# Three pairs of FFN blocks by seven products, two weight sums by adding transfers, another end and narrower masks in a decoder layer in float32

## The chip, the cores and the metric

The kernel runs on one core of a Trainium2 chip. What counts is the device time of one execution in microseconds (us). The core's engines each have their own instruction queue, worked off in order: TensorE (PE, its weight loads PEld), VectorE (DVE), ScalarE (ACT), GpSimd (POOL) and SyncE (SP, which here only issues transfers). Engines wait for each other by semaphores.

## The reference

One decoder layer on x of 256 positions and width 1024, all in float32: a half-step SwiGLU FFN, then attention in parallel with a gated MLP, then a second half-step FFN, a final norm; shift, scale and gate of each part come from a product of the conditioning vector c with `w_ada`.

```python
y = modulate(rmsnorm(h, norm_ffn2[l]), sh3, sc3)
h = h + 0.5 * gt3[:, None, :] * swiglu(y, w_ffn2_gu[l], w_ffn2_down[l])
return rmsnorm(h, norm_final)

def swiglu(x, w_gu, w_down):
    g, u = jnp.split(x @ w_gu, 2, axis=-1)
    return (jax.nn.silu(g) * u) @ w_down
```

The hidden width of an FFN is 2816. Sequence length equals the attention's block, so attention is causal within the 256 positions.

## The kernel before, in words

**Tiles.** The 256 positions are two tiles of 128 rows (t = 0, 1). A product in float32 is made of three TensorE products of a reduced type: each operand is split into a high part (a ScalarE copy into that type) and a low part (what is left, a VectorE subtraction), and high·high, low·high and high·low are summed in PSUM (`mm3`). A weight piece is 128 rows by 1024 columns (512 KB). SP loads it into one of 8 `raw` buffers (RBUFS), ScalarE writes `wh`, VectorE `wl`, of which there are 10 each (WBUFS). The pieces of `w_ada` (`ada`) use the same `raw` buffers.

**The second FFN** (`f2`) goes over 11 blocks of 256 hidden columns (NB). For each block there is a part that makes gate and up, an activation (silu on ScalarE, product on VectorE), a split of the result into `ah` and `al` (`turn`), and `down(b)`, 24 matmuls of 512 columns that add the block's share to four PSUM banks `po`. A plain block (`gate_up`) is 16 groups of six matmuls of 256 columns in banks `pg` and `pu`. The blocks named in PAIRS (line 33: 5 and 8) and the block after each are made together (`pair`, lines 549 to 614) by Strassen's scheme: with weights cut into quarters 11, 21 (first block, upper and lower half of the rows) and 12, 22 (second block), seven products P1, P5, P6, P2, P7, P3, P4 stand for eight. Each is 12 matmuls of 512 columns in one of three banks pA, pB, pC. P1, P6 and P7 accumulate in the same bank pA, and between them ScalarE copies it out (`copy`, line 571: u1 after P1, u2 after P6, u3 after P7), so P6 waits for u1 and P7 for u2. Silu for a pair's tiles is `gated` (line 576). A pair's results lie in another layout, so `turn` has TensorE transpose them (four transposes a block) before the split. The sums of activation parts that Strassen's scheme needs (`sum_y`: two VectorE instructions and a ScalarE copy each, four sums) are made once, in the plain blocks that `due` (line 1216) names.

**A pair's weights** (`add_pair`, lines 227 to 291): for each product and each half q of its rows, `prep` loads what is still needed, makes the weight sum by `minus` in place on VectorE (two for P5, four for P6, two after P2, for both q together), and `hi` writes the high part (line 242); `lo` writes the low part. Product n+1 is prepared before the low part of n. After P7 and after P4 a plain `down` follows (`pair_downs`), whose weights stand between the pair's.

**What sets the order.** While TensorE's instructions are written, `tick` calls `fillers` (line 391) whenever a model clock of VectorE is less than LEAD ahead of TensorE's: that issues the next weight, if fewer than WBUFS are live, or the next item of the conditioning (`fill`), at most one piece of `w_ada` per GAP. Each item puts its load on SP's queue, its high part on ScalarE's and its low part on VectorE's. Eight pieces of the last gate (`acc`) are summed by VectorE during the second FFN.

**The end** (lines 1240 to 1270): the downs of the last three blocks (HOLD) are done tile by tile and half by half (t, n). For the very last half the last block goes into two banks `pe` of 256 columns; `add` scales, adds to h, squares and multiplies with the final norm's row.

**Masks.** A causal mask of 128 by 128 (`make_mask`, lines 179 to 185) is added to the attention scores by a matmul with the identity; for t = 1 `maskr` holds a zero half ahead of it, so that the matmul writes all 512 columns of the bank (`step_sc`, line 1079).

## Time and profile before

| | |
|---|---|
| median of 3 runs | 500.62 us (500.24 to 501.04) |
| the profiled execution's own time | 500.92 us |
| its span, first to last instruction | 499.2 us |
| granted TensorE clock, mean | 0.994 of full speed |
| busy | TensorE 98%, VectorE 82%, ScalarE 56%, GpSimd 5% |
| data moved by transfers | 126.46 MB, mean 253 GB/s |

A profile is one execution. A busy share is the share of the span in which an engine worked on an instruction; consecutive records of VectorE and ScalarE overlap by a few hundredths of a microsecond, so n instructions in a row take a little less than n times one. The second FFN with its downs runs from about 310 us to 491 us of the span.

### The profile page before, as it was taken

The page shows a single profiled execution, that of the slowest core. Times are in us where ns is not written, and L with a number is a line of the kernel's source. Part 1 is how long each engine was busy: PE and PEld are TensorE (multiplying, and loading weights), DVE is VectorE, ACT ScalarE, POOL GpSimd, SP SyncE. Part 2 cuts the span into 40 slices and gives each one's busy share as a digit, 9 for nine tenths or more (in the row PEclk, how much of TensorE's full clock was granted, in tenths as well). Part 3 has the DMA queues.
Part 4 walks back from the last instruction along what each step waited for, and adds up shares of the span by engine and source line. Part 5 has one row for each costly group of instructions (what it writes and reads, how often), then busy time and mean ns, then how long its engine had stood idle before and what let it go on. Part 6 is the DMA issues. An engine that isn't in the chain of part 4 may idle for free.

```text
span 499.2 us, 7816 instructions
## 1 busy us (share of the span) xinstructions
PE 487.7 (98%) x2959; PEld 431.6 (86%) x2959; DVE 411.6 (82%) x537; ACT 277.9 (56%) x412; POOL 23.6 (5%) x36
## 2 busy tenths in 40 slices
PE   8999999999999999999999999999999999999993
PEld 6999998999999997887788988889998789788982
DVE  5999989897778557799888999879898879988345
ACT  5656775553544443775676447855536663766221
POOL 4000000000000200100003221000000000000000
PEclk9999999999999999999999999999999999999997
DMA  8999979998899975569776767697901982294002
GB/s 285 404 398 397 399 235 349 410 396 294 315 331 339 337 260 173 178 195 334 242 269 240 228 199 287 214 324 269 352 0 49 341 314 97 93 350 149 0 1 84
DMA packets 38023, 126.46 MB, mean 253 GB/s; under 512 B 4449, under 2 KB 4449, under 8 KB 37986
## 3 DMA queue, kind: packets, MB, share of 16 engines
q1 hardware_dynamic: 37458, 125.39, 70.2%
q10 hardware_dynamic: 432, 0.57, 0.3%
q8 instruction: 23, 0.38, 0.3%
q14 instruction: 14, 0.11, 0.1%
q0 software_dynamic: 96, 0.01, 0.0%
HBM read 124.91 MB, written 1.05 MB: 252 GB/s over the span
## 4 chain that ended last, share of the span: by engine, by line
PE 83%; DVE 7%; issue 4%; ACT 3%; DMA 3%; POOL 0%; POOLq 0%; ACTq 0%; DVEq 0%; SPq 0%
PE po L82 19%; PE pg L82 17%; PE pu L82 13%; PE f L82 6%; PE pw L82 4%; PE pA L82 3%; PE pp_gv L82 2%; PE pp_v L82 2%; PE pp_q L82 2%; PE pp_k L82 2%; PE pp_gu L82 2%; PE psc L82 2%; DMA raw_first<-in_gu_dram 2%; DVE raw_gu L82 1%; DVE wl_gu_5P L82 1%
## 5 line engine op out<-in xcount | busy, mean ns | idle before, releaser
L82 DVE TENSOR_TENSOR wl_gu<-raw_gu,wh_gu 128x1024 fp32r<-128x1024 f32 x56 | 66.9, 1221 | 11.5 <-ACT wh_gu L203 11.3
L203 ACT ACTIVATE wh_gu<-raw_gu 128x1024 fp32r<-128x1024 f32 x56 | 57.3, 1054 | 25.0 <-PE po L82 15.3
L82 PE MATMUL po<-wh_d,ah 128*128 128x512 f32 x174 | 68.3, 392 | 0.2 <-ACT ah L522 0.2
L82 PE MATMUL po<-wl_d,ah 128*128 128x512 f32 x174 | 68.4, 393 | 0.0
L82 PE MATMUL po<-wh_d,al 128*128 128x512 f32 x174 | 68.2, 392 | 0.0
L82 DVE TENSOR_TENSOR wl_d<-raw_d,wh_d 128x1024 fp32r<-128x1024 f32 x44 | 53.4, 1225 | 13.3 <-ACT wh_d L203 13.3
L203 ACT ACTIVATE wh_d<-raw_d 128x1024 fp32r<-128x1024 f32 x44 | 45.8, 1054 | 28.3 <-PE pu L82 10.3
L82 PE MATMUL pu<-yh,wh_gu 128*128 128x256 f32 x192 | 54.3, 283 | 0.3 <-DVE a L82 0.2
L82 PE MATMUL pg<-yh,wh_gu 128*128 128x256 f32 x192 | 54.5, 284 | 0.0
L82 PE MATMUL pu<-yh,wl_gu 128*128 128x256 f32 x192 | 54.4, 283 | 0.0
L82 PE MATMUL pg<-yh,wl_gu 128*128 128x256 f32 x192 | 54.4, 283 | 0.0
L82 PE MATMUL pu<-yl,wh_gu 128*128 128x256 f32 x192 | 54.2, 283 | 0.0
L82 PE MATMUL pg<-yl,wh_gu 128*128 128x256 f32 x192 | 54.2, 282 | 0.0
L82 PEld LDWEIGHTS po<-wh_d,al 128*128 128x128 f32 x174 | 32.7, 188 | 7.5 <-DVE al L82 0.4
L82 PEld LDWEIGHTS po<-wh_d,ah 128*128 128x128 f32 x174 | 32.7, 188 | 7.2 <-ACT ah L522 0.4
L82 DVE SCALAR_TENSOR_TENSOR ada<-ada,c_row 128x1024 f32<-128x1024 f32 x32 | 38.6, 1219 | 0.0
L82 PEld LDWEIGHTS po<-wl_d,ah 128*128 128x128 f32 x174 | 32.7, 188 | 6.6
L82 PEld LDWEIGHTS pu<-yh,wh_gu 128*128 128x128 f32 x192 | 36.3, 189 | 0.8 <-DVE a L82 0.4
L82 PEld LDWEIGHTS pg<-yh,wh_gu 128*128 128x128 f32 x192 | 36.3, 189 | 0.5
L82 PEld LDWEIGHTS pg<-yl,wh_gu 128*128 128x128 f32 x192 | 36.2, 188 | 0.5
L82 PEld LDWEIGHTS pu<-yh,wl_gu 128*128 128x128 f32 x192 | 36.2, 189 | 0.0
L82 PEld LDWEIGHTS pg<-yh,wl_gu 128*128 128x128 f32 x192 | 36.2, 189 | 0.0
(321 smaller groups left out, 1090.4 us busy)
## 6 DMA issues: line engine op xcount, KB each, us to landing
raw_gu<-in_gu_dram SPq DMA_DIRECT2D x72, 512.0 KB, 5.4
raw_d<-in_w_ffn_down_dram SPq DMA_DIRECT2D x44, 512.0 KB, 5.0
ada<-in_w_shsc_dram SPq DMA_DIRECT2D x32, 512.0 KB, 5.2
ada<-in_w_gate_dram SPq DMA_DIRECT2D x24, 512.0 KB, 5.5
raw_ada<-in_w_shsc_dram SPq DMA_DIRECT2D x16, 512.0 KB, 7.2
raw_first<-in_gu_dram SPq DMA_DIRECT2D x16, 512.0 KB, 7.5
raw_wo<-in_w_out_dram SPq DMA_DIRECT2D x8, 512.0 KB, 4.9
raw_inq<-in_w_in_dram SPq DMA_DIRECT2D x4, 512.0 KB, 5.5
```

The lines of the kernel that those rows point to most:

```text
L82: return getattr(self.engine, name)(out, *args, **kw)
L203: nc.scalar.activation(wh[:, :n], raw[:, :n], AF.Copy)
```

## The change

Pairs are now blocks 3+4, 6+7 and 9+10; 0, 1, 2, 5 and 8 are plain. In a pair's weights, the sums 22 − 12 (for P7) and 21 − 11 (for P4) are made by `less`: ScalarE negates a raw quarter in place (line 257) and GpSimd issues a transfer from one raw buffer to the other that adds (line 258); there are 12 of these in all. VectorE keeps four subtractions per pair of eight. Quarter 22 is loaded with P5's, 21 with P6's, and P4 uses the buffers of 11 rather than those of 21. All four activation sums are made in block 2. At the end, block 8 alone is left for `po` in the last half, and blocks 9 and 10 go into the two `pe` banks, twelve matmuls each; the turns of blocks 9 and 10 stand among the last downs. The mask matmul writes only the 128 columns per head of the tile's own keys, so for t = 1 it has 256 columns in place of 512 (four instructions), and `maskr` loses its zero half with the VectorE instruction that made it. The program has 98 matmuls and transposes fewer (rows of the order, 2802 to 2704), VectorE 483 to 489 instructions, ScalarE 347 to 370, GpSimd 41 to 53, SP 248 as before.

```diff
--- before.py
+++ after.py
@@ -30,7 +30,7 @@
 RBUFS = 8
 HOLD = 3
 AHEAD = 4
-PAIRS = (5, 8)
+PAIRS = (3, 6, 9)
 STRASSEN = ("P1", "P5", "P6", "P2", "P7", "P3", "P4")
 LEAD = 1
 GAP = 3
@@ -174,15 +174,14 @@
     vec.tensor_scalar(onesr, ident, 0.0, 1.0, op0=ALU.mult, op1=ALU.add)
     identr = const.tile([P, P], F32R, name="identr")
     vec.tensor_copy(identr, ident)
-    maskr = const.tile([P, 2, P], F32R, name="maskr")
+    maskr = const.tile([P, P], F32R, name="maskr")
 
     def make_mask():
         mask = op.tile([P, P], F32, name="mask", bufs=1)
         nc.gpsimd.memset(mask, 0.0)
         nc.gpsimd.affine_select(out=mask, in_=mask, pattern=[[-1, P]], base=0,
                                 channel_multiplier=1, compare_op=ALU.is_ge, fill=NEG)
-        vec.tensor_scalar(maskr[:, 0, :], mask, 0.0, None, op0=ALU.mult)
-        vec.tensor_copy(maskr[:, 1, :], mask)
+        vec.tensor_copy(maskr, mask)
 
 
 
@@ -253,18 +252,25 @@
         def minus(to, x, y, q):
             vec.tensor_tensor(part[to, q], part[x, q], part[y, q], op=ALU.subtract)
 
+        def less(to, x, q):
+
+            nc.scalar.activation(part[to, q], part[to, q], AF.Copy, scale=-1.0)
+            nc.gpsimd.dma_start(part[to, q], part[x, q], accum_op=ALU.add)
+
         def prep(key, q):
 
-            if q == 0 and key in ("P1", "P5", "P6", "P2"):
-                load(*{"P1": ("11", b, 0), "P5": ("12", b + 1, 0), "P6": ("22", b + 1, 1), "P2": ("21", b, 1)}[key])
+            if q == 0:
+                for name, blk, half in {"P1": (("11", b, 0),), "P5": (("12", b + 1, 0), ("22", b + 1, 1)),
+                                        "P6": (("21", b, 1),)}.get(key, ()):
+                    load(name, blk, half)
             if key == "P5":
                 minus("11", "12", "11", q)
+                less("12", "22", q)
             elif key == "P6":
-                minus("12", "22", "12", q)
                 minus("11", "22", "11", q)
             hi(place[key], key, q)
 
-        place = dict(zip(STRASSEN, ("11", "11", "11", "21", "12", "22", "21")))
+        place = dict(zip(STRASSEN, ("11", "11", "11", "21", "12", "22", "11")))
         order = [(key, q) for key in STRASSEN for q in range(2)]
 
         def item(n):
@@ -275,8 +281,8 @@
                     prep(*order[n + 1])
                 key, q = order[n]
                 lo(place[key], key, q)
-                if key == "P2":
-                    minus("21", "21", "11", q)
+                if key == "P6":
+                    less("11", "21", q)
             return run
 
         for n, (key, q) in enumerate(order):
@@ -1082,13 +1088,16 @@
         hb, par, h0 = sc_of(t, q)
         p = p_sc[t, q] = psa(f"psc{t}{q}").rearrange("p (h n) -> p h n", h=hb)
         rs = slice(par * DH, (par + 1) * DH)
-        mk = maskr.rearrange("p a b -> p (a b)")[:, 2 * P - nk:]
-        ten.matmul(p, identr, mk[:, None, :].to_broadcast([P, hb, nk]), start=True, stop=False)
+
+
+        ten.matmul(p[:, :, tsl(t)], identr, maskr[:, None, :].to_broadcast([P, hb, P]), start=True, stop=False,
+                   skip_group_check=True)
         for hh in range(hb):
             hd = h0 + 2 * hh + par
             for kk in range(t + 1):
                 ten.matmul(p[:, hh, tsl(kk)], qkT[0, t][rs, hd // 2, :],
-                           qkT[1, kk][rs, hd // 2, :], start=False, stop=(hh == hb - 1 and kk == t))
+                           qkT[1, kk][rs, hd // 2, :], start=False, stop=(hh == hb - 1 and kk == t),
+                           skip_group_check=True)
 
     def step_mx(t, q):
         once(("mx", t, q), ("sc", t, q))
@@ -1213,7 +1222,7 @@
         sums_y[m] = (zh, zl)
 
     waiting = [0, 1]
-    due = {2: [1], 3: [3], 4: [2, 4]} if min(PAIRS) > 4 else {2: [1, 3], 3: [2, 4]}
+    due = {2: [1], 3: [3], 4: [2, 4]} if min(PAIRS) > 4 else {2: [1, 3], 3: [2, 4]} if min(PAIRS) > 3 else {2: [1, 3, 2, 4]}
     for b in range(2, NB):
         if b in PAIRS:
             f2.pair(b, waiting, pair_downs(b))
@@ -1243,22 +1252,23 @@
 
         for n in range(2):
             apart = (t, n) == (NT - 1, 1)
-            for b in range(NB - HOLD, NB - 1 if apart else NB):
+            for b in range(NB - HOLD, NB - 2 if apart else NB):
                 if b == NB - 2 and last not in f2.a:
                     f2.turn(last)
                 for k in range(2):
-                    end = b == NB - 2 and k == 1 if apart else None
+                    end = b == NB - 3 and k == 1 if apart else None
                     run(f2.down_ops(b, k, t, end)[3 * n:3 * n + 3])
             add(n, f2.po[t][n], slice(0, 512), not apart)
         if apart:
             for q in range(2):
                 o = slice(q * 256, q * 256 + 256)
                 pe = psm(f"pe{q}")[:, 0:256]
-                for k in range(2):
-                    ah, al = f2.a[last]
-                    wh, wl = need(("d2", last, k))
-                    mm3(pe, ah[:, k, tsl(t)], al[:, k, tsl(t)], wh[:, 512 + o.start:512 + o.stop],
-                        wl[:, 512 + o.start:512 + o.stop], k == 0, k == 1)
+                for b in (NB - 2, NB - 1):
+                    for k in range(2):
+                        ah, al = f2.a[b]
+                        wh, wl = need(("d2", b, k))
+                        mm3(pe, ah[:, k, tsl(t)], al[:, k, tsl(t)], wh[:, 512 + o.start:512 + o.stop],
+                            wl[:, 512 + o.start:512 + o.stop], (b, k) == (NB - 2, 0), (b, k) == (NB - 1, 1))
                 add(1, pe, o)
             v = sm.tile([P, 1], F32, tag="var", name=f"v2_z{t}")
             vec.tensor_tensor(v, c.parts[0], c.parts[1], op=ALU.add)
```

The order of instructions follows from `fillers`. Three places show it. Names: `wh_gu2_5P31` is the high part for pair 5, product P3, second half (q = 1); `raw_gu2_6110` the raw quarter 11 of pair 6, first half; `u1_25` the copy u1 of pair 5; `d2_3_0` the first weight of block 3's down.

ScalarE in the second half of a pair's weights: before, pair 5 (line 571 is the copy of bank pA, 242 a pair's high part, 203 another weight's, 522 the split of a turned block).

```order
L242 ACTIVATE wh_gu2_5P21_4144<-raw_gu2_5211_4124 128x1024
L242 ACTIVATE wh_gu2_5P70_4160<-raw_gu2_5120_3963 128x1024
L242 ACTIVATE wh_gu2_5P71_4179<-raw_gu2_5121_3965 128x1024
L242 ACTIVATE wh_gu2_5P30_4186<-raw_gu2_5220_4002 128x1024
L571 ACTIVATE u1_25_4193<-pA25_4171 128x512
L522 ACTIVATE ah_24_4195<-a_24_4134 128x512
L203 ACTIVATE wh_d2_3_0_4206<-raw_d2_3_0_4205 128x1024
L203 ACTIVATE wh_d2_3_1_4218<-raw_d2_3_1_4217 128x1024
L242 ACTIVATE wh_gu2_5P31_4229<-raw_gu2_5221_4004 128x1024
L242 ACTIVATE wh_gu2_5P40_4236<-raw_gu2_5210_4122 128x1024
L571 ACTIVATE u2_25_4243<-pA25_4171 128x512
```

Now, pair 6 (577 the copy, 241 and 202 the high parts, 257 the negation).

```order
L241 ACTIVATE wh_gu2_6P20_4253<-raw_gu2_6210_4200 128x1024
L257 ACTIVATE raw_gu2_6111_4098<-raw_gu2_6111_4098 128x1024
L241 ACTIVATE wh_gu2_6P21_4265<-raw_gu2_6211_4202 128x1024
L241 ACTIVATE wh_gu2_6P70_4277<-raw_gu2_6120_4115 128x1024
L241 ACTIVATE wh_gu2_6P71_4287<-raw_gu2_6121_4117 128x1024
L241 ACTIVATE wh_gu2_6P30_4294<-raw_gu2_6220_4119 128x1024
L577 ACTIVATE u1_26_4298<-pA26_4272 128x512
L528 ACTIVATE ah_25_4300<-a_25_4228 128x512
L202 ACTIVATE wh_d2_4_0_4323<-raw_d2_4_0_4322 128x1024
L202 ACTIVATE wh_d2_4_1_4335<-raw_d2_4_1_4334 128x1024
L241 ACTIVATE wh_gu2_6P31_4343<-raw_gu2_6221_4121 128x1024
L577 ACTIVATE u2_26_4347<-pA26_4272 128x512
```

Ahead of u1 stand four high parts (P2's second half, both of P7, one of P3) as before, and now a negation ahead of those; between u1 and u2 stand the two weights of a down, as before, and one high part of the pair in place of two.

VectorE between two pairs: before, after pair 5.

```order
L82 TENSOR_TENSOR wl_d2_4_0_4275<-raw_d2_4_0_4273,wh_d2_4_0_4274 128x1024
L82 TENSOR_TENSOR wl_d2_4_1_4287<-raw_d2_4_1_4285,wh_d2_4_1_4286 128x1024
L82 TENSOR_TENSOR u3_25_4291<-u3_25_4291,pC25_4172 128x512
L82 TENSOR_TENSOR u3_25_4291<-u3_25_4291 128x256
L82 TENSOR_TENSOR wl_gu2_7_0_4319<-raw_gu2_7_0_4317,wh_gu2_7_0_4318 128x1024
L82 TENSOR_TENSOR wl_gu2_7_1_4327<-raw_gu2_7_1_4325,wh_gu2_7_1_4326 128x1024
L82 TENSOR_TENSOR wl_gu2_7_2_4338<-raw_gu2_7_2_4336,wh_gu2_7_2_4337 128x1024
L82 TENSOR_TENSOR wl_gu2_7_3_4356<-raw_gu2_7_3_4354,wh_gu2_7_3_4355 128x1024
L82 TENSOR_TENSOR wl_d2_5_0_4368<-raw_d2_5_0_4366,wh_d2_5_0_4367 128x1024
L82 TENSOR_TENSOR u2_25_4243<-u2_25_4243,pC25_4172 128x512
L82 TENSOR_TENSOR u2_25_4243<-u2_25_4243 128x256
L82 TENSOR_TENSOR wl_d2_5_1_4383<-raw_d2_5_1_4381,wh_d2_5_1_4382 128x1024
```

Now, after pair 3.

```order
L82 TENSOR_TENSOR wl_d2_2_0_3957<-raw_d2_2_0_3955,wh_d2_2_0_3956 128x1024
L82 TENSOR_TENSOR wl_d2_2_1_3970<-raw_d2_2_1_3968,wh_d2_2_1_3969 128x1024
L82 SCALAR_TENSOR_TENSOR acc8_3401<-ada8_4_3977,cols_79,acc8_3401 128x1024
L82 TENSOR_TENSOR wl_gu2_5_0_3988<-raw_gu2_5_0_3986,wh_gu2_5_0_3987 128x1024
L82 TENSOR_TENSOR u2_23_3877<-u2_23_3877,pC23_3809 128x512
L82 TENSOR_TENSOR u2_23_3877<-u2_23_3877 128x256
L82 TENSOR_TENSOR wl_gu2_5_1_4006<-raw_gu2_5_1_4004,wh_gu2_5_1_4005 128x1024
L82 TENSOR_TENSOR u4_23_4013<-u4_23_4013,pA23_3808 128x256
L82 TENSOR_TENSOR wl_gu2_5_2_4022<-raw_gu2_5_2_4020,wh_gu2_5_2_4021 128x1024
L82 SCALAR_TENSOR_TENSOR acc8_3401<-ada8_5_4031,cols_79,acc8_3401 128x1024
L82 TENSOR_TENSOR wl_gu2_5_3_4041<-raw_gu2_5_3_4039,wh_gu2_5_3_4040 128x1024
L82 TENSOR_TENSOR wl_d2_3_0_4053<-raw_d2_3_0_4051,wh_d2_3_0_4052 128x1024
```

Steps of `acc8`, the summing of the last gate, now stand between the weights there; before, all of them came ahead of the first pair.

TensorE where the last gate and up ends: before.

```order
L82 MATMUL pu210_4883<-yh_109,wh_gu2_10_3_4796 128x256
L82 MATMUL pu210_4883<-yl_110,wh_gu2_10_3_4796 128x256
L82 MATMUL pu210_4883<-yh_109,wl_gu2_10_3_4797 128x256
L82 MATMUL po200_3757<-wh_d2_8_0_4808,ah_28_4931 128x512
L82 MATMUL po200_3757<-wl_d2_8_0_4809,ah_28_4931 128x512
L82 MATMUL po200_3757<-wh_d2_8_0_4808,al_28_4932 128x512
L82 MATMUL po200_3757<-wh_d2_8_1_4823,ah_28_4931 128x512
```

Now.

```order
L82 MATMUL pA29_4749<-wl_gu2_9P41_4827,yh_109 128x512
L82 MATMUL pa_29_4948<-ident_99,u1_29_4773 128x128 x2
L82 MATMUL pa_29_4948<-ident_99,u4_29_4945 128x128 x2
L82 MATMUL po200_3774<-wh_d2_8_0_4836,ah_28_4775 128x512
L82 MATMUL po200_3774<-wl_d2_8_0_4837,ah_28_4775 128x512
L82 MATMUL po200_3774<-wh_d2_8_0_4836,al_28_4776 128x512
L82 MATMUL po200_3774<-wh_d2_8_1_4851,ah_28_4775 128x512
L82 MATMUL po200_3774<-wl_d2_8_1_4852,ah_28_4775 128x512
L82 MATMUL po200_3774<-wh_d2_8_1_4851,al_28_4776 128x512
L82 MATMUL pa_210_4965<-ident_99,u2_29_4821 128x128 x2
L82 MATMUL pa_210_4965<-ident_99,u3_29_4871 128x128 x2
```

Before, a plain block (`pu210`) stood ahead of the last downs; now P4 of pair 9 stands there, and the transposes of block 9, the second two of which read u4, which is made from P4's bank, come right behind it.

## Rows read from the trace of the kernel before

**Rows 1.** The page's part 1: busy us (share of the span), instructions, of each engine.

```profile
PE 487.7 (98%) x2959; PEld 431.6 (86%) x2959; DVE 411.6 (82%) x537; ACT 277.9 (56%) x412; POOL 23.6 (5%) x36
```

**Rows 2.** Table by stretches: PE, PEld, DVE, ACT, POOL busy; PEclk, DMA share, GB/s.

```profile
341.00:358.00 17.00, 17.00 (x123) 16.00 (x122) 16.04 (x17) 8.73 (x10) 0.00 (x0) 1.00 0.92 341
...
358.00:390.00 32.00, 32.00 (x190) 28.30 (x189) 28.22 (x29) 17.07 (x21) 0.00 (x0) 1.00 0.25 77
...
390.00:414.00 24.00, 23.81 (x106) 19.11 (x105) 19.85 (x22) 15.90 (x22) 0.00 (x0) 1.00 0.92 338
```

**Rows 3.** Chain of waits from 330 to 500 us: start, us, what.

```profile
341.73 5.51 PE po L82 x24
...
348.68 0.72 PE pg L82 x6
...
385.57 3.39 DMA raw_d<-in_w_ffn_down_dram
...
392.02 0.49 ACT u L571
...
431.91 2.79 PE pA L82 x12
...
466.64 0.44 PE pa L82 x4
```

**Rows 4.** VectorE's timeline, second FFN: start, duration, engine, operation, [idle before, releaser].

```profile
327.35 1.22 DVE L82 TENSOR_TENSOR wl_gu<-raw_gu,wh_gu 128x1024 fp32r<-128x1024 f32 x1
...
329.44 0.42 DVE L82 TENSOR_TENSOR a<-sg,pg 128x256 f32<-128x256 f32 x1 [0.87 <-ACT sg L500]
...
338.70 0.69 DVE L82 TENSOR_TENSOR s1l<-y_f,s1h 128x512 fp32r<-128x512 f32 x1 [0.70 <-ACT s1h L1211]
...
339.31 1.28 DVE L82 SCALAR_TENSOR_TENSOR acc<-ada,cols,acc 128x1024 f32<-128x1024 f32 x1
...
378.89 1.22 DVE L82 TENSOR_TENSOR wl_gu_5P<-raw_gu,wh_gu_5P 128x1024 fp32r<-128x1024 f32 x1
...
391.30 4.62 DVE L82 TENSOR_TENSOR wl_gu_5P<-raw_gu,wh_gu_5P 128x1024 fp32r<-128x1024 f32 x4
...
413.39 0.41 DVE L82 TENSOR_TENSOR u<-u,pA 128x256 f32<-128x256 f32 x1
...
427.05 2.35 DVE L82 TENSOR_TENSOR wl_gu_8P<-raw_gu,wh_gu_8P 128x1024 fp32r<-128x1024 f32 x2
```

**Rows 5.** TensorE's timeline: the first matmul of P1 of pair 5.

```profile
381.14 0.40 PE L82 MATMUL pA<-wh_gu_5P,yh 128*128 128x512 f32 x1
```

**Rows 6.** ScalarE's timeline, pair 5.

```profile
384.13 0.60 ACT L571 ACTIVATE u<-pA 128x512 f32<-128x512 f32 x1 [0.52 <-PE pA L82]
...
390.03 1.99 ACT L242 ACTIVATE wh_gu_5P<-raw_gu 128x1024 fp32r<-128x1024 f32 x2
...
412.89 0.36 ACT L576 ACTIVATE u<-pA 128x256 f32<-128x256 f32 x1
```

**Rows 7.** DMA issues: queue, count, KB each, median us from issue to landing.

```profile
raw_gu<-in_gu_dram SPq DMA_DIRECT2D x72, 512.0 KB, 5.4
...
acc<-in_b_ada_dram POOLq DMA_DIRECT2D x3, 4.0 KB, 4.8
```

**Rows 8.** TensorE's groups from 240 to 262 us: the mask's matmuls (t = 1).

```profile
L82 PE MATMUL psc<-maskr,identr 128*128 128x512 f32 x4 | 1.8, 445 | 0.0
```

**Rows 9.** VectorE's timeline at the end.

```profile
489.80 0.69 DVE L82 TENSOR_TENSOR res_z<-po,ada_row 128x512 f32<-128x512 f32 x1 [0.60 <-PE po L82]
...
491.13 0.42 DVE L82 TENSOR_TENSOR res_z<-pe,ada_row 128x256 f32<-128x256 f32 x1
...
492.38 0.42 DVE L82 TENSOR_TENSOR res_z<-pe,ada_row 128x256 f32<-128x256 f32 x1
```

**Rows 10.** GpSimd's timeline, 280 to 320 us.

```profile
297.38 1.46 POOL L415 TENSOR_TENSOR r_f<-v_f,mhalf 128x1 f32<-128x1 f32 x1 [9.80 <-DVE v_f L82]
...
310.35 0.56 POOL L415 TENSOR_TENSOR r_f<-v_f,mhalf 128x1 f32<-128x1 f32 x1 [9.72 <-DVE v_f L82]
```

## The prediction

> **What bounds the kernel now.** The page's first part comes first: TensorE is busy 98% of the span, VectorE 82%, ScalarE 56% [rows 1]. So a TensorE instruction removed is a gain only as long as the split weights arrive in time, and 82% is an average that has to be read stage by stage. The table by stretches does that for the second FFN [rows 2]: between 341 and 414 us TensorE is busy without a gap that counts, while VectorE is busy 16.04 of 17 us, 28.22 of 32 and 19.85 of 24. TensorE leads, and VectorE follows close behind with little room. How close, the timelines show. In pair 5 the low part of P6's second half starts on VectorE at 378.89 and ends at 380.1 [rows 4]; TensorE starts P1 of that pair at 381.14 [rows 5], so VectorE is 1.0 us ahead of P1. For pair 8 the same low part ends at 428.2 [rows 4] and P1 starts at 431.91 [rows 3]: 3.7 ahead. The one place where this lead was too short is in the chain: P7 of pair 5 waited for ScalarE's copy u2 of bank pA (392.02, 0.49 us [rows 3]). That copy stands in ScalarE's order behind weights' high parts [rows 6], one of which waited for its load (385.57, 3.39 us [rows 3]). The same order is kept by the change, so this is the place to watch.
>
> **What TensorE saves.** All of this is against the profiled execution, 500.92 us with a span of 499.2; it lies 0.3 above the median of the three runs and inside their spread, so no correction is made.
> - A plain block is 16 groups of six matmuls at 0.72 us, a product twelve at 2.79 [rows 3]. Two plain blocks, 32 × 0.715 = 22.9, become seven products, 19.5: −3.4. Two more blocks are turned by four transposes, 0.44 each [rows 3]: +0.9.
> - Four mask matmuls [rows 8] shrink from 512 to 256 columns, from 0.23 us (2.79/12) to 0.12 (0.72/6): −0.45. The VectorE instruction dropped from the opening is worth nothing beside other work there.
> - The end: six 512-column matmuls of `po` go into the two `pe` banks, so `po` ends 6 × 0.23 = 1.4 us earlier and VectorE's work on it (from 489.80) is done before the first `pe` arrives. TensorE's own end stays. The second piece starts on VectorE at 492.38 now, behind the first at 491.13 [rows 9]; it can start some 0.3 us after TensorE's last matmul, at about 491.15: −1.2.
> - Block 9's turn now stands right behind P4 of the last pair, and its operand is P4's own result: silu 0.36 on ScalarE [rows 6], product 0.41 on VectorE [rows 4], with handoffs about 1.1, less two transposes that are ready: +0.9. Before, a plain block stood in between.
>
> Sum: −3.4 + 0.9 − 0.45 − 1.2 + 0.9 = −3.3, or **497.6** if nothing comes late.
>
> **What the splitting costs.** Prices on VectorE, each less the 0.08 us by which its records overlap: 1024 columns 1.14 (four in 4.62, one alone 1.22), an `acc` step 1.20, 512 columns 0.61, 256 columns 0.34 [rows 4]. A high part on ScalarE is about 1.0, a copy of a bank 0.6 [rows 6].
>
> *Pair 3.* TensorE reaches P1 when block 2 and the downs of block 0 are done, 341.73 + 5.51 = 347.24 [rows 3] (0.45 earlier with the masks, for both engines alike), and ends P5 at 352.8. From 327.35 VectorE has ten instructions of 1024 columns, eleven of 512 and one of 256 up to and with P6's second low part: 11.4 + 6.7 + 0.35 = 18.45. All four activation sums are now among them. The waits it has now stay: 0.87 for the silu, 0.70 for ScalarE in each of four sums [rows 4], some 1.1 for high parts: 4.8. It is done at 350.6, 3.4 **after** P1's start where pair 5 had 1.0 before it. ScalarE can only then negate that half, and P2's and P7's high parts are queued ahead of copy u1: 3 × 1.0 + 0.6 and a handoff, 354.3. P6 accumulates in bank pA, so it waits for u1: stall 1.5.
>
> P7 waits for u2, and u2 stands behind the high part of the first weight of block 1's down. That weight's load takes the raw buffer which the fourth adding transfer reads. (Behind it in SP's queue stand that down's second weight and block 2's, which are read only after P7.) Negation done 351.7, the transfer L, the load 3.4 [rows 3], high part 1.0, copy 0.6, handoffs 0.5: 357.2 + L, against the end of P2 at 359.9. Stall L − 2.7.
>
> *L* has no row. A transfer issued by GpSimd takes 4.8 us to land even for 4 KB [rows 7]; 512 KB at the 341 GB/s of that stretch [rows 2] is 1.5 more. I take 6.3. Bounds: 3.4, a load by the other queue [rows 3], below; 4.8 + 5.4 = 10.2 [rows 7] above. With 6.3 the stall is 3.6. The Trainium skill, "DMA: Bandwidth & Descriptors", section "Anatomy of one DMA — SWDGE (gpsimd) path", puts a transfer on this path at 2.0 us plus bytes/436e3, by my estimate 3.2 for 512 KB; by that the total below would be 501.1. The 4.8 of rows 7, where it would give 2.0, speak against it here.
>
> *Pair 6.* From 350.6 VectorE has 28 × 1.14 + 5 × 1.20 (the `acc` steps now fall between pairs 3 and 6) + 7 × 0.61 + 4 × 0.34 = 43.5 until P6's second low part. Its idle share was 13% of its busy time at 358 to 390 and 21% at 390 to 414 [rows 2]: 5.8 to 9.1, so done between 399.9 and 403.2. TensorE: seven products, three downs, block 5 with two turns and the stalls so far, 347.24 + 19.5 + 16.5 + 12.3 + 5.1 = 400.7 for P1, 406.3 for P6. Here six ScalarE instructions stand from that low part to u1 (negation, four high parts, copy), 5.7 us: u1 at 405.6 to 408.9, stall 0 to 2.6, taken 1.5. P7's u2 stands behind the second weight of block 4's down, whose load waits for the eighth adding transfer, and one more high part: stall L − 3.7 = 2.6.
>
> *Pair 9.* No `acc` step is left and VectorE is ahead by several us, as in pair 8: nothing. The sums for P7 and P3 (first two transfers of a pair) have over 15 us until they are read, and VectorE's four subtractions saved per pair are in the counts. GpSimd itself has nothing else queued until the end.
>
> Stalls: 1.5 + 3.6 + 1.5 + 2.6 = 9.2. **497.6 + 9.2 = 506.8.**
>
> **The rivals.**
> - A, late splits as worked out. With L = 4.8 the two P7 stalls are 3.2 together and the total 503.8; with 10.2, where the first long stall gives VectorE back its lead before pair 6, about 510.5. Chance 0.58.
> - B, all hidden: **faster**, 497.6. It decides at pair 3: if P6's second low part is done no later than some 0.5 us after P1's start, u1, the negation and the load behind the transfer move up by 3 us and both stalls there are gone. For it: VectorE could draw ahead before 327, where no pair stands in its way. Against it: the tight stretch at 341 to 358 [rows 2]. Chance 0.28.
> - C, cheap transfers: L = 3.4, like a load. Stalls 1.5 + 0.7 + 1.5 + 0 = 3.7, **501.3**, near no change. Chance 0.08.
> - D, transfers held up: GpSimd's `r_f` took 1.46 us beside VectorE's `ada` steps and 0.56 elsewhere [rows 10]. If what GpSimd does for a transfer stretches likewise, 4.8 × 2.6 + 1.5 = 14, the P7 stalls are 11.3 and about 4, the total **514**. The Trainium skill, "SBUF — State Buffer", section "Who interferes with whom", says that a VectorE instruction with two inputs in SBUF contends with a GpSimd instruction that reads SBUF; the 1.46 agrees, and whether it holds for issuing a transfer no row shows. Chance 0.06.
>
> **How the numbers follow.** The likeliest is A: 506.8. A alone spans 503 to 511. The range 497 to 511.5 takes in A, C and most of B; it leaves out D, the part of B below 497 and A's tails, together under 0.2. About 0.2% of 500.6, 1 us to either side, is what a measurement of this kernel tells from no change. Faster: B and a little of C, 0.30; within it: half of C and the low edge of A, 0.06; slower: 0.64.
>
> **What would show it.** TensorE idle before P6 and P7 of pairs 3 and 6, with ScalarE's `u` as releaser, and none in pair 9; ahead of the P7 copies a ScalarE `wh_d` that waits for a load; the adding transfers landing about 6 us after issue; 2.79 us per product and a last VectorE chain that starts at once behind TensorE. Wrong would be: no idle TensorE in pair 3 (B), transfers of 3 us or of over 10 (C, D), or a stall on another releaser, the transfers' results themselves above all.

## The result and the profile after

The changed kernel takes **514.31 us** (median of 4 runs, 513.86 to 516.27) against 500.71 for the kernel before on the same chip: a ratio of 1.0278, with a 95% interval of 1.0265 to 1.0292. The forecast was 506.8, the range 497 to 511.5. So the sign was right and the size was not: +13.6 us in place of +6. The profiled execution took 514.54 us, span 512.8.

The page's part 1, which answers to [rows 1]:

```profile
PE 489.7 (95%) x2865; PEld 426.6 (83%) x2865; DVE 416.7 (81%) x543; ACT 296.7 (58%) x435; POOL 34.4 (7%) x48
```

TensorE's busy share fell from 98 to 95%: with fewer instructions it is busy 2 us longer, and in 23.1 us of the span (512.8 - 489.7) it does nothing, where it was 11.5 before. Where it waits shows TensorE's weight-load queue, timeline (start, duration, engine, operation, and in brackets the idle time before and its releaser):

```profile
354.21 0.19 PEld L82 LDWEIGHTS pA<-wh_gu_3P,s2h 128*128 128x128 f32 x1 [2.30 <-ACT u L577]
...
363.12 0.19 PEld L82 LDWEIGHTS pA<-wh_gu_3P,s3h 128*128 128x128 f32 x1 [1.94 <-ACT u L577]
...
410.91 0.29 PEld L82 LDWEIGHTS pA<-wh_gu_6P,s2h 128*128 128x128 f32 x1 [5.32 <-ACT u L577]
...
419.48 0.19 PEld L82 LDWEIGHTS pA<-wh_gu_6P,s3h 128*128 128x128 f32 x1 [0.80 <-ACT u L577]
...
426.93 0.19 PEld L82 LDWEIGHTS pada<-acch,onesr 128*128 128x128 f32 x1 [2.09 <-ACT acch L333]
...
466.85 0.19 PEld L82 LDWEIGHTS pA<-wh_gu_9P,s2h 128*128 128x128 f32 x1 [1.27 <-ACT u L577]
...
487.93 0.20 PEld L82 LDWEIGHTS pa<-ident,u 128*128 128x128 f32 x2 [0.95 <-DVE u L82]
```

Rows 1 and 2 are P6 and P7 of pair 3, rows 3 and 4 those of pair 6, all released by ScalarE's copies `u` of bank pA, as the forecast had it. Row 5 is new: the row of the last gate (`pada`), waiting for ScalarE's split of its sum. Row 6 is P6 of pair 9, row 7 the new turn at the end. What follows a wait can be slow, too. The table by stretches (PE, PEld, DVE, ACT, POOL busy; PEclk; DMA share; GB/s) of P6 and the product behind it, in pair 3 and in pair 6:

```profile
354.20:358.60 4.40, 4.39 (x12) 3.47 (x13) 3.89 (x4) 2.37 (x3) 0.00 (x0) 0.61 0.72 167
358.60:361.40 2.80, 2.80 (x13) 2.08 (x12) 0.27 (x1) 0.00 (x0) 0.00 (x0) 1.00 0.78 272
...
410.90:416.10 5.20, 5.19 (x12) 4.13 (x13) 2.14 (x3) 0.95 (x2) 0.00 (x0) 0.50 0.97 331
416.10:419.10 3.00, 3.00 (x13) 2.07 (x11) 2.29 (x2) 2.74 (x4) 0.00 (x0) 1.00 0.81 230
```

P6 of pair 6 ran at a granted clock of 0.50, the lower of the two levels, and took 5.2 us in place of 2.79 [rows 3]; P6 of pair 3 at 0.61. The chain of waits shows what stood ahead of the copies (start, us, what):

```profile
350.72 1.07 ACT raw_gu L257
...
352.08 6.10 DMA raw_gu<-raw_gu
...
358.24 3.27 DMA raw_d<-in_w_ffn_down_dram
361.53 1.06 ACT wh_d L202
362.58 0.48 ACT u L577
...
405.55 1.04 ACT raw_gu L257
406.59 3.79 ACT wh_gu_6P L241 x4
410.37 0.49 ACT u L577
...
410.91 5.41 PE pA L82 x12
```

In pair 3: negation, adding transfer (6.1 us), the load that waits for its buffer, that weight's high part, copy u2. In pair 6: negation, four high parts, copy u1, and P6 in 5.41. VectorE's timeline gives the times at which it was done:

```profile
349.41 2.35 DVE L82 TENSOR_TENSOR wl_gu_3P<-raw_gu,wh_gu_3P 128x1024 fp32r<-128x1024 f32 x2
...
362.62 1.23 DVE L82 TENSOR_TENSOR wl_d<-raw_d,wh_d 128x1024 fp32r<-128x1024 f32 x1 [3.75 <-ACT wh_d L202]
...
402.32 2.44 DVE L82 TENSOR_TENSOR wl_gu_6P<-raw_gu,wh_gu_6P 128x1024 fp32r<-128x1024 f32 x2
```

The first of the two at 349.41 is P6's second low part in pair 3, done at 350.6. At 362.62 VectorE had stood 3.75 us for the same late load's high part. The second of the two at 402.32 is P6's second low part in pair 6, done at 404.8, where P1 had started at 400.3.

What stood ahead of rows 5 and 6 of TensorE's weight-load queue, from VectorE's and ScalarE's timelines (line 582 is `gated`, a pair's silu):

```profile
414.33 1.28 DVE L82 SCALAR_TENSOR_TENSOR acc<-ada,cols,acc 128x1024 f32<-128x1024 f32 x1 [2.23 <-DMA ada<-in_w_gate_dram]
...
425.94 0.42 ACT L582 ACTIVATE u<-u 128x256 f32<-128x256 f32 x1 [1.73 <-DVE u L82]
426.26 1.13 ACT L333 ACTIVATE acch<-acc 128x512 fp32r<-128x512 f32 x2
...
456.08 2.35 DVE L82 TENSOR_TENSOR wl_gu_9P<-raw_gu,wh_gu_9P 128x1024 fp32r<-128x1024 f32 x2
...
465.25 1.06 ACT L202 ACTIVATE wh_d<-raw_d 128x1024 fp32r<-128x1024 f32 x1 [2.53 <-DMA raw_d<-in_w_ffn_down_dram]
```

The last summing step of the gate waited 2.23 us for its load, but it was done at 415.6. The split of the sum (426.26) stands on ScalarE behind a silu of pair 6 (425.94), and that waited for VectorE, which had worked with one gap of 0.5 us since 416.7. In pair 9 P6's second low part is the first of the two at 456.08: it is done at 457.3, 3.0 us before P1 (460.26). VectorE is not late there. Copy u1 stands behind a down's weight (465.25) that waited 2.53 us for its load, and SP had issued this load at 460.29, when the pair's third adding transfer (issued at 455.25) had landed.

The transfers themselves (DMA issues: count, KB, median us from issue to landing):

```profile
raw_gu<-raw_gu POOLq DMA_DIRECT2D x12, 512.0 KB, 4.9
```

Put together, from the starts of the products in TensorE's timeline, each against an unbroken sequence:

| place | forecast | measured |
|---|---|---|
| pair 3: wait before P6, slow P6, wait before P7 | 1.5, 0, 3.6 | 2.0, 1.7, 1.7 |
| pair 6: wait before P6, slow P6, wait before P7 | 1.5, 0, 2.6 | 5.1, 2.5, 0.5 |
| pair 6: row of the last gate, wait for its high part, for its low part | 0 | 1.8, 0.7 |
| pair 9 and the down behind it | 0 | 1.5 |
| sum | 9.2 | 17.5 |

With the forecast's 497.6 for all the rest these 17.5 us make 515.1, 0.6 above the profiled execution.

At the end VectorE's timeline, for [rows 9]:

```profile
502.68 0.69 DVE L82 TENSOR_TENSOR zo<-h,nfin 128x512 f32<-128x512 f32 x1
503.29 0.68 DVE L82 TENSOR_TENSOR res_z<-po,ada_row 128x512 f32<-128x512 f32 x1
...
504.62 0.42 DVE L82 TENSOR_TENSOR res_z<-pe,ada_row 128x256 f32<-128x256 f32 x1
...
505.87 0.42 DVE L82 TENSOR_TENSOR res_z<-pe,ada_row 128x256 f32<-128x256 f32 x1
```

### The profile page after: what moved, and what is told of

Same layout as the page of the kernel before. It is cut to its first block, busy times and chain, and to the rows that moved or that the text cites. A ratio compares the mean times of both kernels' runs of the same rounds, so it can differ in the third digit from the quotient of the medians.

```text
span 512.8 us, 7699 instructions
## 1 busy us (share of the span) xinstructions
PE 489.7 (95%) x2865; PEld 426.6 (83%) x2865; DVE 416.7 (81%) x543; ACT 296.7 (58%) x435; POOL 34.4 (7%) x48
## 4 chain that ended last, share of the span: by engine, by line
PE 67%; DVE 14%; DMA 7%; ACT 6%; issue 5%; SPq 0%; POOL 0%; POOLq 0%; ACTq 0%; DVEq 0%
PE po L82 15%; PE pg L82 13%; PE pu L82 9%; PE f L82 6%; PE pw L82 4%; DMA raw_first<-in_gu_dram 3%; PE pp_gv L82 2%; PE pp_v L82 2%; PE pp_q L82 2%; PE pp_gu L82 2%; PE pp_k L82 2%; DVE raw_gu L82 2%; DVE wl_d L82 2%; DVE wl_gu_3P L82 2%; PE pA L82 2%
## 5 line engine op out<-in xcount | busy, mean ns | idle before, releaser
L82 DVE TENSOR_TENSOR wl_gu<-raw_gu,wh_gu 128x1024 fp32r<-128x1024 f32 x48 | 57.6, 1221 | 9.5 <-ACT wh_gu L202 9.2
L202 ACT ACTIVATE wh_gu<-raw_gu 128x1024 fp32r<-128x1024 f32 x48 | 49.2, 1053 | 22.0 <-PE po L82 13.9
L82 PE MATMUL pg<-yh,wh_gu 128*128 128x256 f32 x160 | 45.5, 285 | 0.0
L82 PE MATMUL pu<-yh,wh_gu 128*128 128x256 f32 x160 | 45.2, 282 | 0.2 <-DVE a L82 0.2
L82 PE MATMUL pu<-yh,wl_gu 128*128 128x256 f32 x160 | 45.3, 283 | 0.0
L82 PE MATMUL pg<-yh,wl_gu 128*128 128x256 f32 x160 | 45.2, 283 | 0.0
L82 PE MATMUL pu<-yl,wh_gu 128*128 128x256 f32 x160 | 45.2, 282 | 0.0
L82 PE MATMUL pg<-yl,wh_gu 128*128 128x256 f32 x160 | 45.1, 282 | 0.0
L82 DVE SCALAR_TENSOR_TENSOR acc<-ada,cols,acc 128x1024 f32<-128x1024 f32 x24 | 30.7, 1279 | 2.3 <-DMA ada<-in_w_gate_dram 2.2
L82 PEld LDWEIGHTS pu<-yl,wh_gu 128*128 128x128 f32 x160 | 30.1, 188 | 0.0
```

Source lines behind the costliest of these rows:

```text
L82: return getattr(self.engine, name)(out, *args, **kw)
L202: nc.scalar.activation(wh[:, :n], raw[:, :n], AF.Copy)
```

## The experiments

Each is an edit of the changed kernel unless it says otherwise; times are medians beside a kernel before of 500.7 to 501.1.

**Two pairs with all the rest of the change.**

```diff
-PAIRS = (3, 6, 9)
+PAIRS = (5, 8)
```


> The changed kernel with pairs 5+6 and 8+9 as before, all else of the change kept (adding transfers, end, masks). Theory (the third pair's place in the order is what costs: loads behind adding transfers hold ScalarE and VectorE where VectorE has no lead): pair 5 has its lead, so about 499.5 us, between 498 and 501. Rival 1 (an adding transfer costs wherever it stands, 12 now, 8 here): the excess of 17 us over the undisturbed sum shrinks to about two thirds, 508 or more. Rival 2 (the end or the masks cost): above 512.

Measured: **498.83 us**, ratio 0.9963 (0.9948 to 0.9978). Eight adding transfers, and TensorE does not wait once in pair 5. Its chain of waits there (start, us, what):

```profile
385.11 2.76 PE pC L82 x12
387.87 2.75 PE pA L82 x12
390.61 2.78 PE pB L82 x12
393.39 2.76 PE pA L82 x12
```

P6's second low part is done at 377.4 there and P1 starts at 382.2: VectorE is 4.7 us ahead. So transfers, masks and end do not cost by themselves. Whether it is the number of pairs or their places that costs, this run alone does not tell. The kernel is faster than both the one before and the changed one.

**Masks and end alone**: two pairs, and all sums on VectorE with loads and buffers as before.

```diff
-PAIRS = (3, 6, 9)
+PAIRS = (5, 8)
...
-                less("12", "22", q)
             elif key == "P6":
+                minus("12", "22", "12", q)
                 minus("11", "22", "11", q)
...
-                if key == "P6":
-                    less("11", "21", q)
+                if key == "P2":
+                    minus("21", "21", "11", q)
```


> Pairs 5+6 and 8+9 with all weight sums on VectorE as before; only the end in two banks and the masks of the own chunk are changed. Theory: the masks take 0.45 us of TensorE and the end 1.2 us of VectorE's last chain away, so 500.7 - 1.65 = 499.0 us (498.6 to 499.6). Rival (the end was hidden anyway, or twelve matmuls per bank bring the last VectorE chain no nearer): 500.2 to 500.7.

Measured: 500.05, ratio 0.9981 (0.9972 to 0.9991): 0.7 less in place of 1.65; the interval reaches 1.4. The end was mis-sized: VectorE is still at the half before (502.68 in the fence above) when `po` is done, takes it at 503.29, and so the second of the last pieces starts 1.25 us after the first (504.62, 505.87), as before. What is gained is 0.7: in TensorE's and VectorE's timelines the last piece starts 1.54 us behind the start of the last matmul before, and 0.86 with two pairs and the new end. The difference between this kernel and the two pairs, 1.2 us, is what the adding transfers, with their order of loads, bring where VectorE has its lead.

**The same sums by VectorE, at the same places.**

```diff
-            nc.scalar.activation(part[to, q], part[to, q], AF.Copy, scale=-1.0)
-            nc.gpsimd.dma_start(part[to, q], part[x, q], accum_op=ALU.add)
+            nc.vector.tensor_tensor(part[to, q], part[x, q], part[to, q], op=ALU.subtract)
```


> The changed kernel with the two sums 22-12 and 21-11 made by one VectorE subtraction each, at the same places in the order, in place of negation and adding transfer. Theory (two things cost alike: VectorE's lateness, and the load that waits for the transfer): VectorE gets 4.6 us more per pair but the load for P7's copy comes some 5 us earlier; pair 3 stalls about 3.5 us in place of 5.4, pair 6 about as now; 511 to 515 us in all. Rival 1 (the adding transfers are the whole cost): at most 506. Rival 2 (VectorE's load alone decides, and transfers cost nothing): above 517.

Measured: 515.46, ratio 1.0295 (1.0279 to 1.0310). The adding transfers are not the whole cost, nor free: what they delay weighs about as much as what they take off VectorE. The total came as forecast, its split did not: pair 3 loses 5.4 us as with the transfers (3.5 expected; P6 waits 3.2, P7 0.5), and pair 6 waits longer before P7 (3.1 us).

**The down's weights later.**

```diff
-            x = {9: 0, 13: 1}.get(n)
+            x = {12: 0, 13: 1}.get(n)
```


> The changed kernel with the first down's weights in a pair placed behind P4's first half in the order of weights, so that ScalarE has the copy u2 and VectorE the low parts of P3 ahead of them; no work is removed or added. Theory (a load that waits for the adding transfer stands in the order of ScalarE, 5.0 us idle, and of VectorE, 3.75 us idle, in pair 3): P7 of pair 3 waits 1.7 us less, P6 of pair 6 some 3.7 us less: about 508.5 us, between 505 and 511. Rival 1 (VectorE's amount of work for three pairs decides, not the waits in its order): 513 to 515. Rival 2 (the clock after a stall is the larger part): 512 or more as long as any stall is left in both pairs.

Measured: **507.65**, ratio 1.0145 (1.0114 to 1.0176), 6.7 less by order alone. The total came as forecast, its split did not: P6 of pair 6 starts only 1.2 us earlier (3.7 expected), but at full clock, and P7 4.1 earlier (415.37 for 419.48), since u2 no longer stands behind the load. These starts are of the profiled execution, the longest of the four (509.92), which was 1.15 us behind already at P6 of pair 3 (355.36 for 354.21). VectorE does not stand 3.75 us in pair 3, and in pair 6 its P6 low part is done 0.9 us behind P1 (403.6 for 402.7) where it was 4.4: P6 waits 1.5 us there in place of 5.1. In pair 3 the wait moved from P7 to the down: TensorE's waits, whole kernel (us in total, times, longest):

```profile
PEld pA L82 <- ACT u L577: 4.1, 2, 2.3
...
PEld po L82 <- DVE wl_d L82: 2.1, 2, 1.1
PEld pada L82 <- ACT acch L333: 1.7, 1, 1.7
...
PEld po L82 <- ACT wh_d L202: 1.2, 2, 0.8
```

**The clock kept up.**

```diff
+            if b in (3, 6):
+                warm = spare[0](f"warm{n}")
+                for x in range({3: 8, 6: 21}[b]):
+                    nc.tensor.matmul(warm, identr, sums_y[1][0].rearrange("p a b -> p (a b)"), start=True, stop=True)
             prod(pa, sums_y[2], "P6", False)
```


> The changed kernel with matmuls on constants into a spare bank ahead of P6, 8 in pair 3 and 21 in pair 6, about as long as TensorE's waits there (2.0 and 5.1 us). The output does not use them. In the changed kernel P6 ran at half the granted clock behind these waits and took 4.45 and 5.25 us in place of 2.79. Theory (P7 waits for copy u2 in any case, which stands behind a load): both P6 take 2.8 us again, but P7 of pair 3 starts where it did (363.1) and P7 of pair 6 at most 0.7 us earlier; the time stays within 1 us of 514.3. Rival (the lower clock costs what it shows): 4.1 us less, 510.2.

Measured: 514.64, ratio 1.0278 (1.0255 to 1.0302), no gain. The table by stretches, the filled wait and P6 of pair 6:

```profile
405.40:410.40 5.00, 5.00 (x24) 3.80 (x22) 4.33 (x4) 5.00 (x7) 0.86 (x1) 1.00 0.97 183
410.40:413.20 2.80, 2.80 (x13) 2.34 (x13) 0.83 (x2) 0.46 (x1) 0.00 (x0) 1.00 0.96 277
```

P6 took 2.8 us at full clock. P7 of pair 3 nevertheless starts only 0.5 us earlier (362.60 for 363.12), and has waited longer:

```profile
354.07 0.19 PEld L82 LDWEIGHTS pA<-wh_gu_3P,s2h 128*128 128x128 f32 x1 [0.51 <-ACT u L577]
...
362.60 0.19 PEld L82 LDWEIGHTS pA<-wh_gu_3P,s3h 128*128 128x128 f32 x1 [3.16 <-ACT u L577]
```

P7 of pair 6 starts at 419.12 for 419.48, and it is now P7 that runs slow (4.4 us); that is taken back in the wait for the gate's row behind it, 0.53 us in TensorE's weight-load queue in place of 2.09. The lower clock is a symptom here: the 4.1 us by which both P6 were slow are time in which P7 would have waited for u2.

**The sums' low parts apart.**

```diff
...
-        vec.tensor_tensor(zl, z, zh.bitcast(F32), op=ALU.subtract)
+        while lows:
+            lows.pop(0)()
+        lows.append(lambda: vec.tensor_tensor(zl, z, zh.bitcast(F32), op=ALU.subtract))
```


> The changed kernel with the low part of each activation sum written behind the next sum's first subtraction, so that VectorE does not wait 0.70 us for ScalarE in each; no work is removed. Theory (VectorE is late at pair 3 by its amount of work and by these waits): P6's second low part 2 us earlier, the stall of 2.0 us before P6 of pair 3 and its slow clock (1.7) nearly gone, the load behind the fourth adding transfer 2 us earlier too, so about 2 to 4 us less: 510 to 512.5. Rival (ScalarE's order alone sets the copies): under 0.7 us less.

Measured: 511.50, ratio 1.0215 (1.0198 to 1.0232), 2.8 less; P6's second low part in pair 3 is done at 347.3 for 350.6, and P6 follows P5 without a wait, at full clock. VectorE's lateness at pair 3 was what held it. P7 of pair 3 still waits 1.8 us, and P6 of pair 6 as long as before (5.0).

**GAP 8, and GAP 8 with the edits of down_late and sums_apart.**

```diff
-GAP = 3
+GAP = 8
```


> The changed kernel with GAP 8 in place of 3, so that one of the last gate's summing steps stands between pairs 3 and 6 and not five. Theory (what VectorE has between pairs 3 and 6 decides the stall before P6 of pair 6, 5.1 us and 2.5 of slow clock behind it): four steps of 1.2 us and their loads go, P6 of pair 6 stalls under 1 us, and the wait for the gate's row (1.8 and 0.7) leaves that place: 505 to 508 us. Rival (TensorE waits there for loads and ScalarE's order, not for VectorE's amount): 512 or more.

> The three together on the changed kernel: the down's weights behind P4's first half (as in down_late), GAP 8, and the sums' low parts apart. Theory: stalls of pair 3 and 6 nearly gone; what is left is the new turn at the end (0.9) and waits of the downs for their weights behind P7: 498 to 502 us. Rival (VectorE's total for three pairs is too much whatever the order): 504 or more.

Measured: 545.85 and 545.61. Both miss, and for a reason of their own: GAP spaces the conditioning of the earlier parts as well, and it came late for them. TensorE's waits in the first of the two:

```profile
PEld pp_k L82 <- ACT yh L672: 10.6, 1, 10.6
...
PEld pg L82 <- ACT yh L672: 6.5, 1, 6.5
```

Their times tell nothing of pair 6. In the first of the two, with one summing step between the pairs, its P6 waits 2.8 us in place of 5.1, but what came before differs too. The next ones leave GAP as it is for all but the last gate.

**Five summing steps left out.**

```diff
+            if comp == 8 and 2 <= k <= 6:
+                return
             raw = wp.tile([P, 1024], F32, tag="raw", bufs=RBUFS, name=f"ada{comp}_{k}")
```


> The changed kernel without five of the eight summing steps of the last gate (steps 2 to 6, their 512 KB loads and their VectorE instructions are left out, so the last gate is only partly summed). Theory (what VectorE has, and what waits for loads, between pairs 3 and 6 decides pair 6): VectorE has 6.0 us less there, and the first down's load in pair 3 takes the buffer of the third adding transfer, not the fourth, so it comes some 6 us earlier. The stall before P7 of pair 3 (1.7) and all of pair 6 (10.7 with slow clock and the wait for the gate's row) go; the stall before P6 of pair 3 (2.0 and 1.7 of slow clock) stays: 500 to 503 us. Rival (three pairs ask too much of VectorE even so): 508 or more.

Measured: 509.86, ratio 1.0180 (1.0163 to 1.0197), far from 500 to 503. VectorE was in time: P6's second low part in pair 6 is the first of the two at 397.84, done at 399.0, 1.5 us before P1 (400.5). Pair 3 kept all its stalls; P7's wait, which should have gone, was 1.9 us.

```profile
397.84 2.35 DVE L82 TENSOR_TENSOR wl_gu_6P<-raw_gu,wh_gu_6P 128x1024 fp32r<-128x1024 f32 x2
...
407.26 1.28 DVE L82 SCALAR_TENSOR_TENSOR acc<-ada,cols,acc 128x1024 f32<-128x1024 f32 x1 [3.77 <-DMA ada<-in_w_gate_dram]
```

P6 of pair 6 still started at 411.21. The step that was left (407.26) waited 3.77 us for its load, the gate's split on ScalarE for the step, and copy u1 stood behind that:

```profile
408.58 1.15 ACT L335 ACTIVATE acch<-acc 128x512 fp32r<-128x512 f32 x2 [4.10 <-DVE acc L82]
```

In the changed kernel this split stood behind pair 6's copies (426.26); the edit has moved it ahead of u1. So the stall here is another one, of the edit's own making, and the run does not tell what VectorE's amount is worth. It shows that whatever stands ahead of a copy in ScalarE's order and waits for a load holds it.

**Copy u1 ahead in ScalarE's order, alone and with steps 2 to 7 left out.**

```diff
+            auto[0] = False
             prod(pa, y(0, 0), "P1", True)
             u1 = copy(pa, "u1")
+            auto[0] = True
```

and, in the second kernel only:

```diff
+            if comp == 8 and k >= 2:
+                return
```


> The changed kernel with no weights issued while P1 of a pair is written, so that copy u1 stands further ahead in ScalarE's order: behind one high part after the last negation in pair 6, not four (and one fewer in pair 3). No work is removed. Theory (ScalarE's order adds to VectorE's lateness): P6 of pair 6 starts 3 us earlier, and with P7 waiting for the same load as before some of it is lost again: 1 to 3 us less, 511.3 to 513.3. Rival (only VectorE's lateness counts, or only the loads): 513.8 or more.

> The changed kernel without summing steps 2 to 7 of the last gate (loads and VectorE instructions left out, the last gate only partly summed) and with copy u1 ahead as in copy_first. In acc_out the second low part of P6 in pair 6 was in time, and u1 stood behind the copy of the gate's sum, which waited for step 7 and its late load. Theory (VectorE's amount between the pairs and ScalarE's order together make the stall before P6 of pair 6): that stall is gone, P6 follows P5; pair 3 keeps its stalls (5.4): 501 to 504 us. Rival (the third pair stalls there for another reason): P6 of pair 6 still over 2 us late, 506 or more.

Measured: 515.02, ratio 1.0268 (1.0234 to 1.0303), and **504.82**, ratio 1.0077 (1.0053 to 1.0101). Alone, the edit moved P6 of pair 6 from 410.91 to 407.27, 3.6 us where 3 were expected, and left 0.2 of the 2.0 us before P6 of pair 3. As P1 of pair 6 came 1.6 us earlier too, the wait before its P6 fell from 5.1 to 2.9. Yet the time is the rival's, no gain, and P1 of pair 9 starts at 459.80 for 460.26: waits for downs behind pair 3, for P7 and for the gate's row took it back. An earlier copy gives VectorE no time: its P6 low part in pair 6 is done at 404.0 for 404.8. With the steps left out as well, P6's second low part in pair 6 (the second of these two on VectorE) is done at 395.9, 3.8 us before P1,

```profile
393.49 2.44 DVE L82 TENSOR_TENSOR wl_gu_6P<-raw_gu,wh_gu_6P 128x1024 fp32r<-128x1024 f32 x2
```

and TensorE goes from P1 through P5 into P6 without a wait (chain, start, us, what):

```profile
399.87 2.79 PE pA L82 x12
402.67 2.80 PE pC L82 x12
405.47 2.79 PE pA L82 x12
```

The time is 0.8 above what was expected: P7 of pair 3 and of pair 9 still wait. But for P6 of pair 6 this is an answer: its wait goes when neither VectorE's lateness (4.4 us behind P1 in the changed kernel) nor ScalarE's order is in the way, and the order alone accounts for 2.1 of the 5.1 us. The steps left out also took six loads away, so VectorE's work and its waits for loads are not told apart.

**Nine raw buffers.**

```diff
-UNITS = 24
+UNITS = 23
...
-RBUFS = 8
+RBUFS = 9
```


> The changed kernel with nine raw buffers in place of eight and 23 buffers for small tiles in place of 24, for space. Theory (the load of the down's first weight waits for the fourth adding transfer because it takes the buffer that this transfer reads): with a ninth buffer it takes another, ScalarE and VectorE do not wait 5.0 and 3.75 us in pair 3, and P6 of pair 6 stalls less: 506 to 510 us. Rival (the buffer is not what these loads wait for): 513 to 516.

Measured: 510.53, ratio 1.0195 (1.0180 to 1.0210), 3.8 less and just above what was expected. P7 of pair 3 follows P2 without a wait, VectorE's idle time there fell from 3.75 to 2.49 us, and P6 of pair 6 starts 1.6 us earlier (409.30 for 410.91). Its wait did not get shorter, as was expected, but is 5.3 us: TensorE comes to P1 1.9 us earlier (398.46 for 400.32).

**Three pairs mended**: the down's weights later, the sums' low parts apart, and a gap of 5 for the last gate's steps alone.

```diff
-                    fill_at[0] = max(fill_at[0], ten.t) + GAP
+                    fill_at[0] = max(fill_at[0], ten.t) + (5 if fill[0][0][1] == 8 else GAP)
```


> The changed kernel with the down's weights behind P4's first half, the sums' low parts apart, and a gap of 5 for the last gate's steps alone (the others keep 3), which leaves three of them between pairs 3 and 6 in place of five. Theory, adding what was measured: 514.3 - 6.7 (down_late) - 2.8 (sums_apart) - 2.4 (two steps) = 502.4, between 500 and 505. Rival (each mended wait is followed by the next, and the parts overlap): 506 to 508, no better than down_late alone.

Measured: **501.06**, ratio 1.0003 (0.9994 to 1.0012), 13 us less than the change and level with before. The gains of the first two edits add up; the gap of 5 was not run alone, so its share is not measured. VectorE's idle time became shorter. From 327 us to P1 of pair 9 (stretch; PE, PEld, DVE, ACT, POOL busy; PEclk; DMA share; GB/s), in the changed kernel:

```profile
327.00:460.26 133.26, 122.53 (x659) 104.25 (x658) 105.52 (x109) 82.50 (x102) 10.51 (x12) 0.96 0.73 223
```

and here:

```profile
327.00:447.32 120.32, 118.16 (x658) 101.39 (x657) 103.97 (x108) 79.59 (x99) 9.63 (x11) 1.00 0.78 244
```

VectorE has 105.5 and 104.0 us of work; it idles 27.7 and 16.4, and TensorE reaches pair 9 13 us earlier. Three pairs at the same places, with the same transfers, cost nothing against before in this order.

**That kernel with copy u1 ahead, and with nine raw buffers too.**

> three_mended2 with copy u1 ahead as in copy_first. In three_mended2 P6 stalled 0.4 us in pair 6 and 0.7 in pair 9 and the first down of pair 3 waited 1.6. Theory: the two stalls before P6 go, 1 us less: 499.5 to 500.5. Rival: what P6 gains P7 or the downs lose, 501.

> three_copy_first with nine raw buffers (and 23 small ones). Theory (the first down of pair 3 waits for the load that waits for an adding transfer): that 1.6 us goes too: 497.8 to 499.5, level with or better than the two pairs' 498.8. Rival (the ninth buffer moves the waits on): 500 or more.

Measured: 509.38, ratio 1.0165 (1.0144 to 1.0185), and 509.67, ratio 1.0171 (1.0146 to 1.0196): both miss, 8 us the wrong way. Holding the weights back during P1 shifts all that follows in the order, and other waits came in the first of them (TensorE's waits: total, times, longest):

```profile
PEld pada L82 <- ACT acch L333: 3.9, 1, 3.9
...
PEld po L82 <- ACT wh_d L202: 2.4, 1, 2.4
```

The ninth buffer does not help then. Three pairs were not brought below two in any order that was tried.

## Why the prediction was wrong

- **Right: the sign, and in pairs 3 and 6 the place and the mechanism.** TensorE waits for copies u1 and u2 there, u2 behind a load that waits for an adding transfer. *Pair 3* was 5.4 us for 5.1. VectorE's P6 low part was done at 350.6, as worked out; the transfer took 6.1 us in the chain for the 6.3 assumed. The Trainium skill, "DMA: Bandwidth & Descriptors", section "Anatomy of one DMA — SWDGE (gpsimd) path", gives 3.2 us by my estimate; the median of 4.9 to landing and the 6.1 in the chain differ, and the measurement decides.
- **Wrong: the step "5.8 to 9.1, so done between 399.9 and 403.2" for pair 6**, and with it the stall of 1.5 before P6, which was 5.1. VectorE was done at 404.8. From 350.6 it was busy 44.5 us by the table by stretches, 1.0 more than the 43.5, and idle 9.7. Of that, 3.75 us is one wait: the load behind the fourth adding transfer was priced for ScalarE's copy alone, but the low part of the same weight stands in VectorE's order. The idle share was taken from stretches of before, which have no load behind an adding transfer. The stall of 1.5 stood for VectorE done at 402.1; the rest of the 3.6 us is ScalarE, 6.1 us from that low part to u1's end for 5.7, and TensorE, due at P6 at 405.85 and not 406.3. In down_late, where VectorE does not have this wait, P6 waits 1.5 us; in acc_order_out, where neither VectorE's lateness nor the order is in the way, not at all.
- **Missing: the row of the last gate**, 2.5 us. The `acc` steps were counted as work. That the split of their sum stands in ScalarE's order behind a silu that waits for VectorE, and that TensorE then waits for the row in the middle of a down, was not followed up.
- **Wrong: pair 9 "nothing"**, 1.5 us. The reason given held, VectorE was 3.0 us ahead of P1; it was not enough. Copy u1 stood behind a load that waited for an adding transfer: 1.0 us before P6, the rest in smaller waits behind it. The forecast had this wait in pairs 3 and 6, for u2, and did not ask for it here.
- **The slow clock** (1.7 and 2.5 us) was in no term. It has to be listed to make the sum come out, but clock_kept took it away and the time stayed: it lies in time that P7 would have waited. With it P7 comes 3.4 us late in pair 3 and 3.0 in pair 6, near the 3.6 and 2.6 of the forecast. So of the 8.3 us that the forecast's waits were short, 3.6 are P6 of pair 6, 2.5 the gate's row, 1.5 pair 9, and 0.7 the small differences elsewhere.
- **The end**: -0.7, not -1.2, for VectorE's queue. The masks' -0.45 was right: the four matmuls of [rows 8] are busy 0.5 us less (group of the same view, count, busy us and mean ns behind the bar):

```profile
L82 PE MATMUL psc<-maskr,identr 128*128 128x256 f32 x4 | 1.3, 332 | 0.0
```

- **The rivals.** B (all hidden) fell with VectorE's low part done at 350.6, 4.0 behind P1 (346.6). In sums_apart its condition (0.5 behind P1) is nearly met, with 0.8, and there only the first of pair 3's two stalls is gone; P7 still waits 1.8 us. C (cheap transfers) fell with the 6.1 us. D gave 514 and was nearly the time measured, for a reason that did not happen: GpSimd's twelve issues took 0.86 to 0.95 us each in its timeline. The Trainium skill's "SBUF — State Buffer", section "Who interferes with whom", is neither borne out nor contradicted for issuing a transfer: the issue at 397.97, beside a VectorE subtraction of two SBUF tiles, took 0.86 us, and so did the one at 392.99, beside none.

What stays open: how the 17.5 us divide by cause. Some of the edits act on the same waits (6.7 us by the order of the weights and 3.8 by a buffer, which both concern the load behind the fourth transfer), and no kernel gives VectorE less work with all results kept.

## What to carry to other kernels

When a transfer is put in the place of arithmetic, follow the buffer that it reads: the next load into that buffer waits for it, and everything behind that load stands still, on each engine on which a piece of it is queued in order. Before trusting a saving on the busiest engine, ask what lead the second busiest has at that place; here the change without its third pair gains 0.4%, because VectorE leads, and with it, at places where VectorE is late, loses 2.8%. And a stall taken away at one place is a gain only if the engine that is late gets time from it: copy_first started P6 3.6 us earlier for nothing, three edits after which VectorE idles 11 us less gave 13 us.

## What the runs showed of the hardware that was not expected

- The granted clock of TensorE falls to 0.50 in the product right behind a wait of 5.1 us, stays there for it (5.2 us for 2.79) and is back at 1.00 in the next. It does not fall behind every wait of a length: behind 2.0 us it was 0.61 in pair 3 of the changed kernel, and in the kernel with nine buffers P6 behind the same 2.0 us took 2.87 us, full speed but for the start; P6 of pair 6 there, behind 5.3 us, had 0.66.
- Matmuls in the wait whose result nothing reads hold the clock at 1.00 (the fence of that kernel); the time is the same, 514.6 for 514.3.
- An adding transfer of 512 KB from one SBUF buffer to another landed in 4.9 us (median), within what loads of that size take (3.4 to 7.5 by tile in the same list), and 4 KB took 5.0 on the same queue.
